# Rows of x and of the second norm turned by VectorE's block transpose and DRAM instead of TensorE

## The chip, the cores and the metric

The kernel runs on one core of a Trainium2 chip. The metric is the device time of one execution in microseconds, the median of several runs. The core's engines have a list of instructions each, worked off in order: TensorE (PE; PEld are its weight loads), VectorE (DVE), ScalarE (ACT), GpSimd (POOL) and SyncE (SP), which issues most DMAs. Lists wait for each other only by semaphores.

## The reference, cut to what matters

One layer of a hybrid decoder on 16 meta tokens and 1024 rows of x, width 1024, all in float32:

```python
u = rmsnorm(h, g_pre_mix)
z = u @ w_in                        # q, k, v, x_rec, y_rec
attn = sliding_window_attention_with_sinks(q, k, v, sinks)
hr = rg_lru(causal_depthwise_conv(xr), ...)
rec = gelu(yr) * hr
h = h + rmsnorm(concat(attn, rec) @ w_out, g_post_mix)
u = rmsnorm(h, g_pre_ffn)           # the second norm
f = square(relu(u @ w_ff1)) @ w_ff2
h = h + rmsnorm(f, g_post_ffn)      # returned without the meta tokens
```

`rmsnorm(x, g)` is x times the reciprocal root of its row's mean square, times g. Both products that begin with `u @` sum over the 1024 columns of u, so u is needed with its columns on the partitions: each tile of 128 rows has to be turned after its norm.

## The kernel before, in words

Each float32 operand of a matmul is split in a high and a low half (`split`, lines 96 and 99: ScalarE's copy to the matmul type, then VectorE's difference), and each product is three matmuls (`mm3`, lines 125, 130, 131): high by high, high by low, low by high.

**The first norm.** The 1040 rows go through in four pieces (`ALL`: 272, then three of 256). `normed` scales the rows of a piece: ScalarE's Square with a row sum (line 254), the reciprocal root as an addition and a power on GpSimd (`rstd_of`, lines 170 and 176), VectorE's multiplication (line 260). `transposed` then turns each of the 8 column blocks by TensorE against the identity into PSUM (line 357), and `split_scaled` multiplies by gamma out of PSUM into the two halves of u (lines 117 and 118). `project` multiplies a piece by a chunk of `w_in` for k, v, q and x_rec; the sinks take the sums from PSUM to SBUF.

**The second norm.** After the attention and the recurrence, `out_mm` forms the product with `w_out` for row tile t (0 to 7) in two PSUM banks. `out_norm` normalises it (Square on ScalarE, line 944; scaling on VectorE, line 950), adds x (line 953), writes the new residual to the output in DRAM (line 954), and scales it by its own norm (lines 956 and 958). `u2_tiles` turns that tile by 8 transposes (line 970) and multiplies by gamma out of PSUM, four blocks on ScalarE (line 981) and four on VectorE (line 975), into `u2f`: per half of four row tiles, four tiles of [128, 2, 512].

**The first feed-forward product** is one level of a fast matrix scheme on 2 by 2 blocks. `operand` splits tiles of `u2f`; `p1` and `p2` are its first products, on the first half of rows (tiles 0 to 3), and are spread between the last tiles' work; `t_sums` forms differences and sums of both halves (`t3`, `t2`), which need all eight tiles, and splits t2 (`ot2`). In the loop that follows, `product(ya[p], wa[p][1], ot2, ...)` is the first use of it. `early` and `prep_a` load and split the weights.

**Order.** The program is written in one order, and the scheduler of the tile framework places each engine's instructions from estimated times; `behind` and `chained` fix a few of them by hand. Buffers come from pools by tag with a fixed count (`raw` 2, `ws` 5, `d` 4, `c` 8 and so on), so a load waits for the last user of its buffer. SP's list holds the loads, the output's writes and, after the change, the trips through DRAM, in one order.

Of the kernel before, what the change touches and what calls it, by code (L numbers as in the profile page):

```python
# [9 lines left out]
F32 = mybir.dt.float32  # L10
# [27 lines left out]
def hybrid_layer(  # L38
# [311 lines left out]
    def transposed(b, xn, after=None):  # L350
        t0, n = ALL[b]
        for kc in range(KC):
            flip[0] += 1
            pt = bank(("pt", "o", "s")[flip[0] % 3])
            o = 0
            for s, m in xn:
                ins = nc.tensor.transpose(
                    pt[:, o : o + m], s[:m, kc * P : (kc + 1) * P], ident[:m, :m]
                )
# [12 lines left out]
            if b == 0:  # L372
                chained(0, high[0])
                chained(1, high[1])

    def fetch(cols, tag="raw", pieces=1):
# [540 lines left out]
    t4_dram = dpool.tile([P, 2, 4, 512], F32, name="t4_dram")  # L917

    u2f = [[None] * 4 for _ in range(2)]

    def out_mm(t, po, kcs):
        half, o = t // 4, (t % 4) * P
# [8 lines left out]
                )  # L931

    def out_banks(t):
        tag = ("pt", "o", "acc", "s", "pt", "acc", "s", "pt")[t]
        return [bank(tag), bank(tag)]

    def out_norm(t, po):
        xr = slot("d", [P, D])
        nc.sync.dma_start(xr, x[t * P : (t + 1) * P, :])
        h = slot("raw", [P, D])  # L940
        ssq = [small.tile([P, 1], F32, name=f"sq{n}", tag=f"sq{n}") for n in range(2)]
        for n in range(2):
            c = slice(512 * n, 512 * n + 512)
            nc.scalar.activation(
                h[:, c], po[n], AF.Square, scale=RMS_SC, accum_out=ssq[n]
            )
        rs = rstd_of(ssq)
        for n in range(2):
            c = slice(512 * n, 512 * n + 512)
            nc.vector.scalar_tensor_tensor(  # L950
                h[:, c], po[n], rs, gmix_b[:, c], op0=ALU.mult, op1=ALU.mult
            )
        nc.vector.tensor_tensor(h, h, xr, op=ALU.add)
# [4 lines left out]
        nc.vector.tensor_scalar(xr, h, rs2, None, op0=ALU.mult)  # L958
        return xr

    def u2_tiles(t, xn):
        half = t // 4
        if u2f[half][0] is None:
            u2f[half] = [slot("c", [P, 2, 512]) for _ in range(4)]
        o = (t % 4) * P
        for k4 in range(0, KC, 4):
            pt = bank("o", (P, 4, P))
            for i in range(4):
                kc = k4 + i
                nc.tensor.transpose(pt[:, i, :], xn[:, kc * P : (kc + 1) * P], ident)  # L970
            for i in range(0, 4, 2):
                kc = k4 + i
                dst = u2f[half][kc // 2]
                if k4:
                    nc.vector.tensor_tensor(
                        dst[:, :, o : o + P], pt[:, i : i + 2, :],
                        g_ffn_col[:, kc : kc + 2].to_broadcast([P, 2, P]), op=ALU.mult,
                    )
                    continue
                for n in range(2):  # L980
                    nc.scalar.activation(
                        dst[:, n, o : o + P], pt[:, i + n, :], AF.Copy,
                        scale=g_ffn_col[:, kc + n : kc + n + 1],
                    )

# [9 lines left out]
    def combine(dst, x0, x1, op):  # L995
        return nc.vector.tensor_tensor(dst, x0, x1, op=op).ins  # L996

    def operand(tiles):
        pairs = []
        for t_ in tiles:  # L1000
            hi, lo = pair("b", [P, 2, 512])
            split(hi, lo, t_)
            pairs.append((hi, lo))
        return pairs

# [106 lines left out]
    for t in range(8):  # L1112
        po = pos[t] if t < 4 else out_banks(t)
        out_mm(t, po, range(6 if t < 4 else 0, KC))
        for t_ in {4: (0,), 5: (2,), 6: (4,), 7: (5,)}.get(t, ()):
            u2_tiles(t_, xns[t_])
        xns[t] = out_norm(t, po)
        for t_ in {4: (1,), 5: (3,), 7: (6,)}.get(t, ()):
            u2_tiles(t_, xns[t_])
        if t == 4:  # L1120
            a11_early.update(early(0, 0, pair("a", ESH)))
        if t == 5:
            b11 = operand(u2f[0][0:2])
# [7 lines left out]
        p1(p, a11_early[p])  # L1131
    for p in range(2):
        p2(p, a12_early[p])
    t3 = [slot("a", [P, 2, 512]) for _ in range(2)]
    t2 = [slot("a", [P, 2, 512]) for _ in range(2)]
    ot2 = [pair("b", [P, 2, 512]) for _ in range(2)]

    def t_sums(c):
        for i in range(2):
            combine(t3[i][:, :, c], u2f[1][2 + i][:, :, c], u2f[1][i][:, :, c], ALU.subtract)  # L1140
            combine(t2[i][:, :, c], t3[i][:, :, c], u2f[0][i][:, :, c], ALU.add)
            hi, lo = ot2[i]
            split(hi[:, :, c], lo[:, :, c], t2[i][:, :, c])
# [9 lines left out]
    p2(2, a12_early[2])  # L1153
    ot3 = [pair("b", [P, 2, 512]) for _ in range(2)]
    for i in range(2):
        behind(urgent, split(*ot3[i], t3[i]))
    wa[1] = prep_a(1, urgent)


    def t_rest(k):  # L1160
        i = k % 2
        if k < 2:
            behind(mark[0], combine(u2f[1][i], u2f[1][i], u2f[0][i], ALU.subtract))
        elif k < 4:
            behind(mark[0], combine(t2[i], u2f[0][2 + i], t2[i], ALU.subtract))
        else:
            hl = pair("a", [P, 2, 512])
            late = mark[0]
            behind(late, split(*hl, t2[i]))
# [339 lines left out]
```

## Time and profile before

| what | us |
|---|---|
| median of 3 runs | 955.24 (955.24 to 955.97) |
| the profiled execution, its span | 955.3 |
| TensorE busy | 943.8 (99%) |
| VectorE busy | 655.7 (69%) |
| ScalarE busy | 505.9 (53%) |
| GpSimd busy | 129.1 (14%) |

The page lists the span as the profiled execution's time, and no other beside it. In rows of instructions the first number is the start in us from the span's start, the second the time to the end of the row's group; a group's row has a count, the busy us and mean ns of one, and the idle time in front with the engine that ended it. A row of a stretch lists busy time and instructions of PE, PEld, DVE, ACT and POOL, then TensorE's granted clock, the DMA engines' share and GB/s. A row of DMA issues gives the count, KB each and median us from issue to landing.

### The profile page before, as it was taken

Reading aid. Unit: us, or ns where it says so; the run is one execution under the profiler, and the core shown is the slowest. Engines: PE = TensorE matmul, PEld = TensorE weight load, DVE = VectorE, ACT = ScalarE, POOL = GpSimd, SP = SyncE. Lnnn points to the kernel's source line nnn. Section 1 sums busy time; section 2 is a strip of 40 time slices with the busy share of each in tenths; the row PEclk is TensorE's granted clock in tenths of the full one; section 3 lists DMA queues with packets and bytes.
Section 4 is the critical chain, followed back from the end, with each engine's and each line's share of the span. In section 5 each row is a group of like instructions: output and inputs, shape, how many; then the busy total and the mean of one; then the engine's idle time right before and its main releaser. Section 6 shows DMA issues by size and latency. Waiting matters only on the chain.

```text
span 955.3 us, 12432 instructions
## 1 busy us (share of the span) xinstructions
PE 943.8 (99%) x4728; PEld 789.7 (83%) x4728; DVE 655.7 (69%) x845; ACT 505.9 (53%) x854; POOL 129.1 (14%) x189
## 2 busy tenths in 40 slices
PE   9999999999999999999999999999999999999996
PEld 8999999877888878888888888888887788888885
DVE  6567987788856787665644465476667576779893
ACT  7537766568645554444655575654433343446441
POOL 4102563520021100010000000001121100001201
PEclk9999999999999999999999999999999999999999
DMA  8221010204226368674422364334777765647934
GB/s 271 56 67 23 24 45 24 67 23 131 83 109 185 133 220 264 198 253 144 155 89 88 111 203 127 104 113 114 175 180 186 185 199 177 192 139 196 246 65 89
DMA packets 88199, 130.21 MB, mean 136 GB/s; under 512 B 13702, under 2 KB 52630, under 8 KB 88140
## 3 DMA queue, kind: packets, MB, share of 16 engines
q1 hardware_dynamic: 78972, 104.44, 34.0%
q0 software_dynamic: 8880, 24.19, 12.2%
q8 instruction: 37, 0.61, 0.3%
q10 hardware_dynamic: 288, 0.79, 0.2%
q14 instruction: 22, 0.18, 0.1%
HBM read 109.93 MB, written 18.87 MB: 135 GB/s over the span
## 4 chain that ended last, share of the span: by engine, by line
PE 88%; DVE 5%; ACT 3%; DMA 2%; POOL 1%; issue 1%; SPq 0%; DVEq 0%; ACTq 0%; POOLq 0%
PE ps_acc L130 10%; PE ps_acc L131 10%; PE ps_acc L125 10%; PE ps_s L131 6%; PE ps_s L130 6%; PE ps_s L125 6%; PE ps_pt L130 6%; PE ps_pt L131 6%; PE ps_pt L125 6%; PE ps_o L130 5%; PE ps_o L131 5%; PE ps_o L125 5%; ACT c L82 1%; PE ps_o L691 1%; PE ps_acc L282 1%
## 5 line engine op out<-in xcount | busy, mean ns | idle before, releaser
L99 DVE TENSOR_TENSOR ws<-raw,ws 128x1024 fp32r<-128x1024 f32 (+1 forms) x69 | 82.6, 1197 | 76.1 <-ACT ws L96 24.3
L96 ACT CAST ws<-raw 128x1024 fp32r<-128x1024 f32 (+1 forms) x68 | 69.7, 1026 | 87.9 <-PE ps_o L130 23.9
L96 ACT CAST ws<-e 128x1024 fp32r<-128x1024 f32 x41 | 43.0, 1049 | 82.8 <-PE ps_o L130 35.3
L125 PE MATMUL ps_acc<-a,ws 128*128 128x256 f32 (+2 forms) x256 | 85.8, 335 | 0.0
L130 PE MATMUL ps_acc<-a,ws 128*128 128x256 f32 (+2 forms) x256 | 85.5, 334 | 0.0
L131 PE MATMUL ps_acc<-a,ws 128*128 128x256 f32 (+2 forms) x256 | 85.0, 333 | 0.0
L99 DVE TENSOR_TENSOR b<-b,b 128x1024 fp32r<-128x1024 f32 (+2 forms) x50 | 58.9, 1177 | 24.8 <-PE ps_o L130 19.1
L96 ACT CAST b<-b 128x1024 fp32r<-128x1024 f32 (+2 forms) x49 | 49.9, 1019 | 46.4 <-DVE b L996 41.0
L99 DVE TENSOR_TENSOR ws<-e,ws 128x1024 fp32r<-128x1024 f32 x41 | 50.1, 1223 | 32.4 <-ACT ws L96 18.9
L680 POOL TENSOR_SCALAR_AFFINE_SELECT c<-c 128x512 fp32r<-128x512 f32 x64 | 53.6, 858 | 67.6 <-ACT c L96 59.3
L125 PEld LDWEIGHTS ps_acc<-a,ws 128*128 128x128 f32 x256 | 48.3, 189 | 4.7 <-issue 0.2
L131 PEld LDWEIGHTS ps_acc<-a,ws 128*128 128x128 f32 x256 | 48.3, 189 | 4.5
L130 PEld LDWEIGHTS ps_acc<-a,ws 128*128 128x128 f32 x256 | 48.2, 188 | 4.4 <-issue 0.4
L125 PE MATMUL ps_acc<-ws,b 128*128 128x512 f32 (+1 forms) x120 | 46.3, 387 | 1.1 <-ACT ws L96 1.1
L130 PE MATMUL ps_acc<-ws,b 128*128 128x512 f32 (+1 forms) x120 | 46.3, 386 | 0.5 <-DVE ws L99 0.4
L131 PE MATMUL ps_acc<-ws,b 128*128 128x512 f32 (+1 forms) x120 | 46.1, 385 | 0.0
L125 PE MATMUL ps_pt<-ws,b 128*128 128x512 f32 x112 | 44.4, 396 | 0.0
L130 PE MATMUL ps_pt<-ws,b 128*128 128x512 f32 x112 | 44.1, 394 | 0.0
L131 PE MATMUL ps_pt<-ws,b 128*128 128x512 f32 x112 | 44.0, 393 | 0.0
L125 PE MATMUL ps_s<-ws,b 128*128 128x512 f32 x110 | 43.4, 395 | 0.0
L131 PE MATMUL ps_s<-ws,b 128*128 128x512 f32 x110 | 43.3, 394 | 0.0
L130 PE MATMUL ps_s<-ws,b 128*128 128x512 f32 x110 | 43.3, 393 | 0.0
(416 smaller groups left out, 2662.0 us busy)
## 6 DMA issues: line engine op xcount, KB each, us to landing
raw<-in_w_ff_dram SPq DMA_DIRECT2D x61, 512.0 KB, 4.1
e<-in_w_ff_dram SPq DMA_DIRECT2D x45, 512.0 KB, 4.0
a<-in_w_ff_dram SPq DMA_DIRECT2D x12, 512.0 KB, 6.6
s_dram<-a POOLq DMA_DIRECT2D x12, 512.0 KB, 3.7
c<-in_x_dram SPq DMA_DIRECT2D x8, 512.0 KB, 4.0
raw<-in_w_in_dram SPq DMA_DIRECT2D x8, 512.0 KB, 3.7
d<-in_x_dram SPq DMA_DIRECT2D x8, 512.0 KB, 3.3
out_dram<-raw SPq DMA_DIRECT2D x8, 512.0 KB
```

The lines of the kernel that those rows point to most:

```text
L82: ins = nc.scalar.activation(*args, **kwargs).ins
L96: nc.scalar.copy(hi, src)
L99: low = nc.vector.tensor_tensor(lo, src, f32(hi), op=ALU.subtract).ins
L125: ins = nc.tensor.matmul(dst, lh, rh, start=start, stop=False, skip_group_check=True).ins
L130: nc.tensor.matmul(dst, lh, rl, start=False, stop=False, skip_group_check=True)
L131: last_mm[0] = nc.tensor.matmul(dst, ll, rh, start=False, stop=stop, skip_group_check=True).ins.name
L282: last_mm[0] = nc.tensor.matmul(acc[:, :n], w[k // 2][:, kc, :], u[kc][k % 2][:, t0 : t0 + n], start=k == 0 and kc == 0, stop=k == last an ...
L680: nc.gpsimd.affine_select(out=p_[:, :, s], in_=f32(p_[:, :, 0]), pattern=[[0, 4], [g, P]], compare_op=op, fill=0.0, base=0, channel_multip ...
L691: nc.tensor.matmul(po[:, oc : oc + n], v, p_[:, pc : pc + n], start=first and k == 0, stop=last and k == 1, skip_group_check=True,)
```

## The change

Three helpers are new. `blocks` turns a scaled tile of 128 by 1024 on VectorE: the hardware turns blocks of 32 by 32, and the read takes every fourth column, so that what lands on one partition goes to DRAM in one run of 4 KB. `unblock` reads it back with the partition that the turned layout wants. `norm_blocks`, `read_blocks` and `split_blocks` use them for the third and fourth piece of x (row tiles 4 to 7), two reads per tile; the first two pieces stay on TensorE. In the second norm, tiles 0 to 6 are multiplied by gamma while they are scaled, against a copy of gamma on every partition (`gpre_b`, one of the five `ws` buffers), turned, written and read back by four reads straight into `u2f`; tile 7 stays on TensorE. `u2f`, t2 and t3 now have the shape [128, 16, 2, 32], and the splits reorder runs of 32 elements (`rows`). The last tile's product moves from the banks `pt` to `o`, which the transposes had used.

```diff
+    def blocks(y, src, dram):
+        nc.vector.transpose(
+            y.rearrange("p (b k t) -> p b k t", b=4, k=KC),
+            src.rearrange("p (k d b) -> p b k d", k=KC, b=4),
+        )
+        nc.sync.dma_start(dram.rearrange("a (d b) r -> (a d) (b r)", b=4), y)
+
+    def unblock(dst, dram, i, n):
+        w = 2 * P // n
+        nc.sync.dma_start(
+            dst.rearrange("p a k t -> p a (k t)"),
+            dram[:, :, w * i : w * i + w].rearrange("a p r -> p a r"),
+        )
+
+    def norm_blocks(b):
+        for i in (2 * b, 2 * b + 1):
+            src, y = xt[i], slot("d", [P, D])
+            ssq = small.tile([P, 1], F32, name="ssq", tag="ssq")
+            nc.scalar.activation(y, src, AF.Square, scale=RMS_SC, accum_out=ssq)
+            rs = rstd_of([ssq])
+            nc.vector.tensor_scalar(src, src, rs, None, op0=ALU.mult)
+            blocks(y, src, x_dram[i - 4])
+
+    def read_blocks(b):
+        for h in range(2):
+            for i in range(2):
+                unblock(turned(b, h)[:, 4 * i : 4 * i + 4], x_dram[2 * b + i - 4], h, 2)
+
+    def split_blocks(b):
+        t0, n = ALL[b]
+        for kc in range(KC):
...
+            split_scaled(
+                uh, ul, turned(b, kc // 4)[:, :, kc % 4], g_mix_col[:, kc : kc + 1]
+            )
...
-        if b:
-            transposed(b, xn if b == 1 else normed(b), done[b])
+        if b == 1:
+            transposed(b, xn, done[b])
+        elif b:
+            split_blocks(b)
+        if b in (1, 2):
+            norm_blocks(b + 1)
+            read_blocks(b + 1)
...
+    LAST_BY_DMA = 6
+    u2_dram = dpool.tile([LAST_BY_DMA + 1, 4, P, 2 * P], F32, name="u2_dram")
+    gpre_b = slot("ws", [P, D])
+    nc.scalar.dma_start(gpre_b, g_pre_ffn[0].partition_broadcast(P))
...
-        tag = ("pt", "o", "acc", "s", "pt", "acc", "s", "pt")[t]
+        tag = ("pt", "o", "acc", "s", "pt", "acc", "s", "o")[t]
...
-        nc.vector.tensor_scalar(xr, h, rs2, None, op0=ALU.mult)
-        return xr
+        if t > LAST_BY_DMA:
+            nc.vector.tensor_scalar(xr, h, rs2, None, op0=ALU.mult)
+            return xr
+        nc.vector.scalar_tensor_tensor(
+            xr, h, rs2, gpre_b, op0=ALU.mult, op1=ALU.mult
+        )
+        blocks(slot("d", [P, D]), xr, u2_dram[t])
...
+    def u2_read(t):
+        g = slice(4 * (t % 4), 4 * (t % 4) + 4)
+        for i, dst in enumerate(u2_half(t // 4)):
+            unblock(dst[:, g], u2_dram[t], i, 4)
...
-        for t_ in {4: (0,), 5: (2,), 6: (4,), 7: (5,)}.get(t, ()):
-            u2_tiles(t_, xns[t_])
         xns[t] = out_norm(t, po)
-        for t_ in {4: (1,), 5: (3,), 7: (6,)}.get(t, ()):
-            u2_tiles(t_, xns[t_])
+        if t:
+            u2_read(t - 1)
...
-    t_sums(slice(0, 3 * P))
+    t_sums(slice(0, 12))
     wa[0] = prep_a(0)
     u2_tiles(7, xns[7])
-    t_sums(slice(3 * P, 4 * P))
+    t_sums(slice(12, 16))
```

More of the change, by code (lines that the diff above doesn't have):

```diff
@@ L374, in transposed, with turned @@
                 chained(1, high[1])
+    def blocks(y, src, dram):
[10 more added lines that the diff above has]
+        )
+    x_dram = dpool.tile([4, 4, P, 2 * P], F32, name="x_dram")
+    def norm_blocks(b):
[6 more added lines that the diff above has]
+            blocks(y, src, x_dram[i - 4])
+    def turned(b, h):
+        return xt[2 * b + h].rearrange("p (g k t) -> p g k t", k=4, t=32)
+    def read_blocks(b):
[5 more added lines that the diff above has]
+        for kc in range(KC):
+            uh, ul = (
+                v[:, t0 : t0 + n].rearrange("p (g t) -> p g t", t=32) for v in u[kc]
+            )
+            split_scaled(
+                uh, ul, turned(b, kc // 4)[:, :, kc % 4], g_mix_col[:, kc : kc + 1]
+            )
     def fetch(cols, tag="raw", pieces=1):
@@ L957, in out_norm, with u2_half @@
         rs2 = rstd_of([ssq2])
-        nc.vector.tensor_scalar(xr, h, rs2, None, op0=ALU.mult)
-        return xr
+        if t > LAST_BY_DMA:
[3 more added lines that the diff above has]
+            xr, h, rs2, gpre_b, op0=ALU.mult, op1=ALU.mult
+        )
+        blocks(slot("d", [P, D]), xr, u2_dram[t])
+    def u2_half(half):
+        if u2f[half][0] is None:
+            u2f[half] = [slot("c", [P, 16, 2, 32]) for _ in range(4)]
+        return u2f[half]
+    def u2_read(t):
+        g = slice(4 * (t % 4), 4 * (t % 4) + 4)
+        for i, dst in enumerate(u2_half(t // 4)):
+            unblock(dst[:, g], u2_dram[t], i, 4)
     def u2_tiles(t, xn):
[L962 to L965, printed above, removed]
+        g = slice(4 * (t % 4), 4 * (t % 4) + 4)
         for k4 in range(0, KC, 4):
@@ L972, in u2_tiles @@
                 kc = k4 + i
[L973 to L979, printed above, removed]
-                for n in range(2):
[L981 to L984, printed above, removed]
+                dst = u2_half(t // 4)[kc // 2]
+                for n in range(2):
+                    d_ = dst[:, g, n]
+                    s_ = pt[:, i + n, :].rearrange("p (a t) -> p a t", a=4)
+                    col = g_ffn_col[:, kc + n : kc + n + 1]
+                    if k4:
+                        nc.vector.tensor_scalar(d_, s_, col, None, op0=ALU.mult)
+                    else:
+                        nc.scalar.activation(d_, s_, AF.Copy, scale=col)
     w1v = w_ff1.rearrange("(b k p) c -> b p k c", b=2, p=P)
@@ L996, in combine, with rows @@
         return nc.vector.tensor_tensor(dst, x0, x1, op=op).ins
+    def rows(tile_, c=slice(0, 16)):
+        return tile_.rearrange("p k (g t) -> p g k t", t=32)[:, c]
     def operand(tiles):
@@ L1001, in operand @@
             hi, lo = pair("b", [P, 2, 512])
-            split(hi, lo, t_)
+            split(rows(hi), rows(lo), t_)
             pairs.append((hi, lo))
@@ L1133, in hybrid_layer @@
         p2(p, a12_early[p])
-    t3 = [slot("a", [P, 2, 512]) for _ in range(2)]
-    t2 = [slot("a", [P, 2, 512]) for _ in range(2)]
+    t3 = [slot("a", [P, 16, 2, 32]) for _ in range(2)]
+    t2 = [slot("a", [P, 16, 2, 32]) for _ in range(2)]
     ot2 = [pair("b", [P, 2, 512]) for _ in range(2)]
@@ L1139, in t_sums @@
         for i in range(2):
-            combine(t3[i][:, :, c], u2f[1][2 + i][:, :, c], u2f[1][i][:, :, c], ALU.subtract)
-            combine(t2[i][:, :, c], t3[i][:, :, c], u2f[0][i][:, :, c], ALU.add)
+            combine(t3[i][:, c], u2f[1][2 + i][:, c], u2f[1][i][:, c], ALU.subtract)
+            combine(t2[i][:, c], t3[i][:, c], u2f[0][i][:, c], ALU.add)
             hi, lo = ot2[i]
-            split(hi[:, :, c], lo[:, :, c], t2[i][:, :, c])
-    t_sums(slice(0, 3 * P))
+            split(rows(hi, c), rows(lo, c), t2[i][:, c])
+    t_sums(slice(0, 12))
     wa[0] = prep_a(0)
     u2_tiles(7, xns[7])
-    t_sums(slice(3 * P, 4 * P))
+    t_sums(slice(12, 16))
     urgent = mark[0]
@@ L1155, in hybrid_layer @@
     for i in range(2):
-        behind(urgent, split(*ot3[i], t3[i]))
+        behind(urgent, split(*map(rows, ot3[i]), t3[i]))
     wa[1] = prep_a(1, urgent)
@@ L1168, in t_rest @@
             late = mark[0]
-            behind(late, split(*hl, t2[i]))
+            behind(late, split(*map(rows, hl), t2[i]))
             for n in range(2):
```

## The prediction

> **What bounds the kernel now.** I read the busy times and the chain that ended last, then busy time by stretch, then the instructions in order of time around the two stages that the change touches, then single groups and DMA times.
>
> ```profile
> PE 943.8 (99%) x4728; PEld 789.7 (83%) x4728; DVE 655.7 (69%) x845; ACT 505.9 (53%) x854; POOL 129.1 (14%) x189
> PE 88%; DVE 5%; ACT 3%; DMA 2%; POOL 1%; issue 1%; SPq 0%; DVEq 0%; ACTq 0%; POOLq 0%
> 20.00:40.00 20.00, 20.00 (x170) 19.64 (x169) 13.77 (x30) 12.06 (x30) 5.11 (x13) 1.00 0.31 81
> 320.00:340.00 20.00, 20.00 (x100) 16.56 (x99) 17.56 (x29) 13.16 (x28) 2.40 (x4) 1.00 0.66 211
> 340.00:360.00 20.00, 19.94 (x86) 15.79 (x85) 15.97 (x26) 10.52 (x17) 1.61 (x3) 1.00 0.56 184
> ```
>
> TensorE is busy 99% at full clock (1.00). A matmul removed is worth its issue slot if nothing else was awaited there, and a wait put in front of TensorE is lost for good, because it has no idle time later to catch up. VectorE is the near second: 17.56 of 20 us in the stretch where the second norm's last tiles become operands.
>
> **The transposes removed.** Per tile of 128 rows TensorE issues 8. Tiles 4 to 7 of x lose 32, tiles 0 to 6 of the second norm 56, in all 88.
>
> ```profile
> 319.31 0.39 PE L131 MATMUL ps_pt<-a,b 128*128 128x512 f32 x1
> 319.54 1.03 PE L970 MATMUL ps_o<-ident,d 128*128 128x128 f32 x8
> 320.33 0.48 PE L125 MATMUL ps_acc<-b,a 128*128 128x512 f32 x1
> 320.64 0.39 PE L130 MATMUL ps_acc<-b,a 128*128 128x512 f32 x1
> ```
>
> Products of 512 columns start 0.23 us apart (319.31, 319.54). Without the transposes the product of 320.64 would have started at 319.77, so 8 transposes cost 0.87 us, 0.109 each, and 88 cost 9.6 us: the largest possible gain, 945.7 us. The Trainium skill ("TensorE: Matmul & The Clock Gate", Part 4) gives some 275 ns for a transpose in a kernel; by that the 88 would be worth 24 us, as an estimate. The trace has that duration (1.03 us ends 0.27 after the last start) but overlaps them, so the step of 0.109 is what counts.
>
> **The x pieces.** Some transposes were free already.
>
> ```profile
> 32.67 0.27 PE L357 MATMUL ps_s<-ident,d 128*128 128x128 f32 x1
> ...
> 33.43 0.38 PE L357 MATMUL ps_o<-ident,d 128*128 128x128 f32 x2
> 33.56 0.36 PE L125 MATMUL ps_acc<-a,ws 128*128 128x256 f32 x1
> 33.05 0.37 ACT L464 COPY c<-ps_acc 128x256 f32<-128x256 f32 x1
> ```
>
> The q product at 33.56 needs the bank that ScalarE's copy of v leaves at 33.42. The 9 transposes in front of it run inside that wait, and the next piece has 8 at the same place. So 17 of 32 are worth nothing; 15 x 0.109 = 1.6 us is gained.
>
> Against it stands VectorE's order. In the changed program its list has the first block transpose right behind the sinks of k of the first piece, ahead of these:
>
> ```profile
> 22.84 0.62 DVE L437 TENSOR_TENSOR ws<-ps_acc,ws 64x144 fp32r<-64x144 f32 x2
> 23.50 1.23 DVE L348 TENSOR_TENSOR ws<-e,ws 128x1024 fp32r<-128x1024 f32 x1
> 25.73 0.48 DVE L118 SCALAR_TENSOR_TENSOR a<-ps_pt,gcol,a 128x256 fp32r<-128x256 f32 x1
> 24.78 1.27 PE L282 MATMUL ps_acc<-a,ws 128*128 128x272 f32 x8
> 26.47 0.36 PE L130 MATMUL ps_acc<-a,b 128*128 128x256 f32 x1
> ```
>
> TensorE's work at 24.78 waits for the low weights that end at 24.73, and that of 26.47 for the first low half of u (26.21). Both move by one block transpose, T.
>
> No row shows T. Bounds from rows of as many columns:
>
> ```profile
> L958 DVE TENSOR_SCALAR d<-raw,rs 128x1024 f32<-128x1024 f32 x8 | 6.0, 754 | 12.8 <-POOL rs L176 12.8
> L953 DVE TENSOR_TENSOR raw<-raw,d 128x1024 f32<-128x1024 f32 x8 | 9.8, 1224 | 0.2
> L851 DVE TENSOR_TENSOR_SCAN c<-b,c 128x1040 f32<-128x1040 f32 x2 | 4.6, 2314 | 0.0
> L1343 DVE SCALAR_TENSOR_TENSOR a<-b,rs,ws 128x1024 f32<-128x1024 f32 x4 | 5.1, 1279 | 0.0
> L975 DVE TENSOR_TENSOR c<-ps_o,gcol 128x256 f32<-128x256 f32 x16 | 6.0, 415 | 0.0
> ```
>
> Fastest 0.75, slowest 2.31; I take 1.22, what most f32 operations of this size take here. So the second piece starts 1.2 us later.
>
> Its u must also be back from DRAM. VectorE turns tile 5 by 31.6 at T = 1.22 (the first low halves end 1.2 later, then a scaling of 0.75 and T); then DMAs:
>
> ```profile
> s_dram<-a POOLq DMA_DIRECT2D x12, 512.0 KB, 3.7
> d<-in_x_dram SPq DMA_DIRECT2D x8, 512.0 KB, 3.3
> raw<-in_w_in_dram SPq DMA_DIRECT2D x8, 256.0 KB, 3.3
> ```
>
> Write 3.7, two reads of 256 KB 3.3 and an issue of 0.4: 39.0 or somewhat later, while TensorE comes to the piece near 40. VectorE reaches its first low half about 0.3 us late. Tiles 6 and 7 have 10 us more. Sum of the x pieces at T = 1.22: -1.6 + 1.2 + 0.3 = -0.1 us. At 0.75: -0.6. At 2.31: VectorE, with four turns and q's sink ahead of those halves, comes 2.0 late: +2.7. The ScalarE and VectorE halves of u keep their count. SP's gate loads queue behind the new DMAs, but are needed only after the attention.
>
> **The second norm.** Each of seven tiles adds on VectorE T and a scaling with gamma of 1.28 for 0.75, and drops two evictions of 0.415: at T = 1.22 a net 0.9 us per tile. ScalarE loses four copies per tile. Four reads of 128 KB in 256-byte runs per tile are added on SP; I take 4.5 us for them, 3.3 and three issues of 0.4. One broadcast of gamma on ScalarE's queue lands long before it is used. The chain of the first tiles:
>
> ```profile
> 269.25 0.76 DVE L958 TENSOR_SCALAR d<-raw,rs 128x1024 f32<-128x1024 f32 x1 [2.12 <-POOL rs L176]
> 270.07 1.41 DVE L950 SCALAR_TENSOR_TENSOR raw<-ps_o,rs,e 128x512 f32<-128x512 f32 x2
> 271.52 1.23 DVE L953 TENSOR_TENSOR raw<-raw,d 128x1024 f32<-128x1024 f32 x1
> 274.92 0.75 DVE L958 TENSOR_SCALAR d<-raw,rs 128x1024 f32<-128x1024 f32 x1 [2.10 <-POOL rs L176]
> ```
>
> The period is 5.67 us with 2.1 idle, waiting for Square and power. The new turn stands ahead of the residual add (L953), not in the idle time, so the period becomes 1.28 + 1.41 + T + 1.23 + 2.1 = 7.2. On SP, tiles 2 to 7's loads of x now stand behind reads that wait for a write (3.7): T turns late, 1 to 2 us more at one or two tiles. Tile 3 is scaled at 292 instead of 286.24, its reads land near 304, and the eight operand splits of tiles 0 to 3 end near 312. None of this stops TensorE: it has the out products of tiles 4 to 7, which end at 315.1 (40 transposes' 4.4 us before 319.54).
>
> Then cover runs out. In the changed order TensorE has 72 products (p1(0), p1(1), p2(0), p2(1), p1(2), p1(3)), tile 7's 8 transposes, two products of p2(2), the first with t2, then ten of p2(2). From 315 that is 16.6 us to the transposes (331.5) and 0.9 + 0.5 to t2 at 332.9. What t2 and p2(2) need, before:
>
> ```profile
> 326.59 0.75 DVE L958 TENSOR_SCALAR d<-raw,rs 128x1024 f32<-128x1024 f32 x1 [0.46 <-POOL rs L176]
> 341.35 0.39 PE L131 MATMUL ps_pt<-b,a 128*128 128x512 f32 x1
> 341.58 0.40 PE L125 MATMUL ps_acc<-b,e 128*128 128x512 f32 x1
> L996 DVE TENSOR_TENSOR a<-c,c 128x768 f32<-128x768 f32 x2 | 1.9, 950 | 0.0
> L996 DVE TENSOR_TENSOR raw<-raw 128x512 f32<-128x512 f32 x16 | 10.9, 688 | 0.3
> L99 DVE TENSOR_TENSOR a<-raw,a 128x1024 fp32r<-128x1024 f32 x6 | 7.3, 1212 | 2.7 <-ACT a L96 2.7
> ```
>
> Tile 7 is scaled near 332 (VectorE's list from tile 4 on takes that long; ScalarE's Square of tile 7 also stands behind the activation of p2(1)'s block, which TensorE finishes at 326). Behind that scaling VectorE has, up to the low half of p2(2)'s weights: five operations of 512 columns (0.69), four new evictions of 128 (0.3, under the 0.415 of 256), five of 768 (0.95), four of 256 (0.42) and one of 1024 (1.21): 12.3 us, 11 with the 0.08 by which neighbours overlap, and 0.6 for a cast: done at 343.6. TensorE waits from 332.9, some 10.7 us. (Those weights cannot come before about 338 in any case: their load waits for tile 7's row to be written out.) It then owes ten products of p2(2), 2.3 us, and is at 345.9 where before it was at 341.8 (p2(2) complete, first t2 product out). So the stage loses 4.1 us, the 6.1 of its 56 transposes being in it already. At T = 0.75 tile 7 comes no earlier than 331.6: +3.7. At T = 2.31 four or five turns are uncovered, tile 7 comes near 337: +9.
>
> **Sum**, against the execution's span of 955.3, equal to the median of 955.24 within 0.1: -0.1 + 4.1 = +4.0, that is 959.3 us. Bounds: 955.3 - 0.6 + 3.7 = 958.4 and 955.3 + 2.7 + 9 = 967.
>
> **Rivals.**
> A slow block transpose. Each read steps over 16 bytes, and if that costs two cycles an element, the price is the scan's 2.31: 967 us. No row of this case reads with such a step, so nothing speaks against it. The Trainium skill ("SBUF — State Buffer", Door 1: The DMA port swizzle) says that SBUF has lines of 16 bytes and that each access to a new line pays a penalty. A step of four f32 is just such an access; no run here shows it yet.
>
> Faster: the cover holds. If VectorE's list behind tile 7 and the load of p2(2)'s weights end by 333 rather than 343.6, the 6.1 us stay, with 1.6 less at most 1.2 in x: 955.3 - 6.1 - 0.4 = 948.8, at best 945.7. It decides at 339.5, where wait and transposes balance. For it: VectorE still has 2.4 us idle in 320 to 340 and loses evictions. Against it: one list in order, where even 1 us of T does not remove the five sums of 768.
>
> Even: only half of that wait comes, 955 to 957.
>
> **Chances.** Forecast 0.46 (own range 957 to 963), slow turn 0.27, cover holds 0.19, even 0.08. A change of 0.2% is about what a measurement tells here: 953.3 to 957.2 is no change. Faster 0.19, same 0.05, slower 0.76. The range 952.5 to 967.5 leaves out most of the cover's case and a tail of the slow one.
>
> **What would show it.** T from its own group. TensorE without L357 after the second piece but with a wait before it near 26; the period of the second norm's first tiles at 7.2 us; a TensorE wait near 332 of about 10 us, released by VectorE's split or ScalarE's cast for p2(2) and t2. The forecast is wrong if TensorE stays at 20.00 in the stretch 320 to 340, or if VectorE's operations on 32-element runs cost more than the 1.21 of contiguous ones.

## The result, and the profile after

The changed kernel takes 977.25 us (median of 4 runs, 974.10 to 982.00) against 955.24 us (955.02 to 955.97): ratio 1.023, with a 95% interval of 1.020 to 1.026. It is 22 us slower, where 4 us had been forecast and no case went beyond 967. The profiled execution of it took 974.1 us, with a span of 972.4 us, 17.1 more than before. It was the fastest of the four, so the sums of waits below account for 17 of the 22 us.

From the page of the changed kernel, busy times and the chain that ended last:

```profile
PE 940.6 (97%) x4640; PEld 784.3 (81%) x4640; DVE 674.1 (69%) x844; ACT 498.9 (51%) x826; POOL 128.7 (13%) x189
PE 81%; DVE 6%; DMA 5%; ACT 3%; issue 2%; POOL 1%; SPq 1%; DVEq 0%; ACTq 0%; POOLq 0%
```

The three stretches of the changed kernel that the prediction showed of the one before:

```profile
20.00:40.00 20.00, 17.86 (x145) 16.83 (x144) 17.90 (x28) 10.99 (x27) 5.55 (x15) 1.00 0.60 175
320.00:340.00 20.00, 18.40 (x77) 13.94 (x76) 16.34 (x17) 7.80 (x16) 3.47 (x6) 1.00 0.71 220
340.00:360.00 20.00, 6.23 (x17) 4.55 (x18) 17.31 (x29) 11.53 (x19) 1.74 (x3) 0.58 0.88 275
```

TensorE's share of the chain fell from 88% to 81%, and DMA has 5% of it. In 340 to 360 us TensorE works 6.23 of 20 us, and for what it does there it was granted 0.58 of its clock. Before, it was 1.00 in all three stretches.

TensorE's waits in the changed kernel, longest first (what waited, for whom, us in all, times, longest):

```profile
PE ps_o L1035 <- DVE d L1012: 7.0, 1, 7.0
PE ps_pt L125 <- ACT a L96: 6.1, 1, 6.1
PE ps_acc L125 <- ACT c L508: 3.6, 1, 3.6
PE ps_acc L282 <- DVE ws L348: 1.8, 1, 1.8
...
PE ps_pt L131 <- DVE a L99: 1.3, 1, 1.3
```

Three of them are in the second norm (7.0 before tile 7's transposes, 6.1 and 1.3 at the first weights behind them), two in the x pieces (3.6 and 1.8). With the small ones they are 24.4 us. The same view of the kernel before begins with this one:

```profile
PE ps_acc L308 <- DVE base_e L562: 1.5, 1, 1.5
```

All its waits together are 4.1 us. To the 20.3 us of difference comes the low clock, 4.3 us (busy time times what is missing to 1.00: 1.3 in 50 to 60 us, 3.0 in 340 to 370 us). Against them stand 71 to 88 removed transposes of 0.109 us, 7.7 to 9.6 (by the prediction 17 of the 88 had stood inside a wait). The sum, 15.0 to 16.9, comes near the 17.1 of the span.

The block transposes and the residual add of the changed kernel, by group:

```profile
L378 DVE STREAM_TRANSPOSE d<-d 128x1024 f32<-128x1024 f32 x7 | 14.0, 2003 | 0.0
L378 DVE STREAM_TRANSPOSE d<-c 128x1024 f32<-128x1024 f32 x4 | 8.1, 2019 | 0.1
L1006 DVE TENSOR_TENSOR raw<-raw,d 128x1024 f32<-128x1024 f32 x8 | 9.8, 1224 | 6.8 <-DMA d<-in_x_dram 6.7
```

VectorE in the changed kernel, in order of time: the scalings of tiles 0 and 1, the add and the scaling of tile 2, and the scaling of tile 7:

```profile
275.01 1.29 DVE L1014 SCALAR_TENSOR_TENSOR d<-raw,rs,ws 128x1024 f32<-128x1024 f32 x1 [2.12 <-POOL rs L176]
282.79 1.29 DVE L1014 SCALAR_TENSOR_TENSOR d<-raw,rs,ws 128x1024 f32<-128x1024 f32 x1 [2.10 <-POOL rs L176]
289.74 1.23 DVE L1006 TENSOR_TENSOR raw<-raw,d 128x1024 f32<-128x1024 f32 x1 [2.44 <-DMA d<-in_x_dram]
293.14 1.29 DVE L1014 SCALAR_TENSOR_TENSOR d<-raw,rs,ws 128x1024 f32<-128x1024 f32 x1 [2.10 <-POOL rs L176]
345.54 0.75 DVE L1012 TENSOR_SCALAR d<-raw,rs 128x1024 f32<-128x1024 f32 x1 [0.46 <-POOL rs L176]
```

A turn takes 2.00 us, not 1.22. The first period of the second norm is 7.78 us (275.01 to 282.79), the next 10.35 (to 293.14), because tile 2's add waits 2.44 us for its load of x. Over the eight tiles the periods are between 7.8 and 12.3 us, and tile 7 is scaled at 345.54 instead of 326.59. Of these 19.0 us, 5.8 are there from the first tile on, which is scaled at 275.01 instead of 269.25: that is the lateness of the x pieces. The longest period, 12.3 us, has no wait for a load of x in it, and the kernel before has one of 12.9 us one tile later (305.49 to 318.37).

### The profile page after: what moved, and what is told of

Its sections match the earlier page's. It is cut to its first block, busy times and chain, and to the rows that moved or that the text cites. A ratio compares the mean times of both kernels' runs of the same rounds, so it can differ in the third digit from the quotient of the medians.

```text
span 972.4 us, 12310 instructions
## 1 busy us (share of the span) xinstructions
PE 940.6 (97%) x4640; PEld 784.3 (81%) x4640; DVE 674.1 (69%) x844; ACT 498.9 (51%) x826; POOL 128.7 (13%) x189
## 4 chain that ended last, share of the span: by engine, by line
PE 81%; DVE 6%; DMA 5%; ACT 3%; issue 2%; POOL 1%; SPq 1%; DVEq 0%; ACTq 0%; POOLq 0%
PE ps_acc L130 10%; PE ps_acc L125 9%; PE ps_acc L131 9%; PE ps_s L131 6%; PE ps_s L130 6%; PE ps_s L125 5%; PE ps_pt L131 5%; PE ps_pt L130 5%; PE ps_pt L125 5%; PE ps_o L130 5%; PE ps_o L131 5%; PE ps_o L125 5%; PE ps_o L740 1%; DMA x_dram<-d 1%; DMA d<-in_x_dram 1%
## 5 line engine op out<-in xcount | busy, mean ns | idle before, releaser
L125 PEld LDWEIGHTS ps_acc<-a,ws 128*128 128x128 f32 x256 | 49.0, 191 | 9.3 <-ACT c L508 4.0
L131 PEld LDWEIGHTS ps_acc<-a,ws 128*128 128x128 f32 x256 | 49.0, 191 | 4.5
L130 PEld LDWEIGHTS ps_acc<-a,ws 128*128 128x128 f32 x256 | 49.0, 191 | 4.4 <-issue 0.4
L130 PE MATMUL ps_pt<-ws,b 128*128 128x512 f32 x110 | 43.4, 395 | 0.0
L131 PE MATMUL ps_pt<-ws,b 128*128 128x512 f32 x110 | 43.3, 394 | 0.0
L125 PE MATMUL ps_pt<-ws,b 128*128 128x512 f32 x110 | 43.2, 393 | 0.0
```

The source lines that it names most:

```text
L125: ins = nc.tensor.matmul(dst, lh, rh, start=start, stop=False, skip_group_check=True).ins
L130: nc.tensor.matmul(dst, lh, rl, start=False, stop=False, skip_group_check=True)
L131: last_mm[0] = nc.tensor.matmul(dst, ll, rh, start=False, stop=stop, skip_group_check=True).ins.name
```

## The experiments

All ratios are to the kernel before, run on the same chip, with 95% intervals. Where several changes are in a run, its diff shows only what is new against the run named.

### Each part alone

The change was cut in two at the second norm: the one run has the new functions and the loop over the pieces of x, and all from `u2f` on as before; the other has x as before and the new second norm.

> Only the pieces 2 and 3 of x go by VectorE's block transposes and DRAM; the second norm is that of the kernel before. In the profile of the changed kernel the first scale of the out norm's chain (the ms of tile 0) stands 5.8 us later than before. Theory A (the two parts' losses add up, since TensorE has no idle time later that could take up the first): 955.2 + 5.8 = 961.0 us, 959.5 to 962.5. Rival B (the lateness is taken up before the second norm, or the x stage disturbs only through the second norm): 954.5 to 957 us.

> Only tiles 0 to 6 of the second norm go by block transposes and DRAM; x is turned by TensorE as before. Theory A (the parts add up): 977.3 - 5.8 = 971.5 us, 969 to 973. Rival B (the second norm's chain is late mainly because the x stage delivers late): under 966 us.

x alone: 963.89 us (961.30 to 968.23), ratio 1.009 (1.006 to 1.012). The second norm alone: 970.57 us (967.82 to 972.75), ratio 1.015 (1.013 to 1.018). The losses are 8.4 and 15.0 us, together 23.4, against 22.0 of both: within the intervals they add up, as theory A had it. But x alone is 1.4 us above theory A's range: it costs 8.4 and not the 5.8 that the profiled execution of the changed kernel showed. A stretch of the run with x alone:

```profile
50.00:60.00 10.00, 6.91 (x38) 6.91 (x39) 4.54 (x19) 3.73 (x10) 0.00 (x0) 0.66 0.01 2
```

ScalarE and TensorE of that run in order of time, in front of that stretch and at its begin:

```profile
48.58 2.50 ACT L117 ACTIVATE a<-c,gcol 128x256 fp32r<-128x256 f32 x6 [3.53 <-DMA c<-x_dram]
50.98 0.73 ACT L477 CAST b<-ps_acc 64x256 fp32r<-64x256 f32 x2
51.73 0.91 ACT L117 ACTIVATE a<-c,gcol 128x256 fp32r<-128x256 f32 x2
52.67 0.37 ACT L508 COPY c<-ps_acc 128x256 f32<-128x256 f32 x1
53.09 0.58 PE L125 MATMUL ps_acc<-a,ws 128*128 128x256 f32 x1 [4.32 <-ACT c L508]
```

ScalarE's list has six of the eight splits of piece 3 (L117), which wait for the reads from DRAM, ahead of the sinks that empty piece 2's banks (L477, the copy of k; L508, that of v). The data come at 48.58, the bank of v is free at 53.04, and TensorE stands 4.3 us. Its granted clock over the stretch of 50 to 60 us is 0.66.

### The turn, read contiguously

```diff
-            src.rearrange("p (k d b) -> p b k d", k=KC, b=4),
+            src.rearrange("p (b k d) -> p b k d", k=KC, b=4),
```

> The same instructions and DMAs as the changed kernel, but each block transpose reads its 32-element runs contiguously instead of with a step of four; the columns then arrive in another order, so the result is that of a permuted operand and only the time is read. Theory S (the step of four makes the block transpose slow): its mean falls from 2.00 us to about 1.2 us, and with 7 turns in the second norm's chain at 0.8 us each and 1.5 us in the x stage the time falls to 968 to 972 us. Rival C (an fp32 block transpose costs 2.0 us however it reads): mean 1.95 to 2.05 us, and the time stays at 975 to 979 us.

978.14 us (975.28 to 978.56), ratio 1.023 (1.021 to 1.025). The group of the second norm's turns in this run, and tile 2's add:

```profile
L378 DVE STREAM_TRANSPOSE d<-d 128x1024 f32<-128x1024 f32 x7 | 8.7, 1239 | 0.0
290.57 1.23 DVE L1006 TENSOR_TENSOR raw<-raw,d 128x1024 f32<-128x1024 f32 x1 [3.45 <-DMA d<-in_x_dram]
```

Theory S is right about the turn and wrong about the time: the step of four costs 0.76 of the 2.00 us, and without it the kernel is not measurably faster. So the turn's price is not what the 22 us are made of. It must stand in front of something that is late anyway, and the second line shows what: tile 2's add now waits 3.45 us for its load of x, where it waited 2.44 behind the slow turns.

### The loads of x ahead of the reads

SP's list in the changed kernel, in order of time:

```profile
287.33 0.33 SPq L382 DMA_DIRECT2D u_dram<-d  x1
290.99 0.34 SPq L1007 DMA_DIRECT2D out_dram<-raw  x1
291.42 2.57 SPq L386 DMA_DIRECT2D c<-u_dram  x4
294.04 0.50 SPq L992 DMA_DIRECT2D d<-in_x_dram  x1
```

The load of x (L992) for the tile after next stands behind the four reads (L386) of a turned tile, and these wait for its write (L382) to land and take 2.6 us to issue. Hence a loop: turn, write, reads, load of x, add, Square, scaling, turn. This run puts the reads of a tile behind the load of x for the tile two further on:

```diff
+        if n == 4:                # in unblock
+            behind(x_load[0], ins)
...
-        nc.sync.dma_start(xr, x[t * P : (t + 1) * P, :])
+        x_load[0] = nc.sync.dma_start(xr, x[t * P : (t + 1) * P, :]).ins.name
...
         xns[t] = out_norm(t, po)
-        if t:
-            u2_read(t - 1)
+        if t > 1:
+            u2_read(t - 2)
...
+    u2_read(6)
```

> The changed kernel, with one change of order on SP's queue: in the second norm the four reads of a turned tile are put behind the load of x for the tile two further on, so that no load of x waits for a write to DRAM to land. Theory Q (the period of 8 to 12 us is the loop turn, write, wait for the landing, reads, load of x, add): the waits of VectorE's adds for x go (2.4, 1.0, 2.5 and 0.8 us in the profile of the changed kernel), tile 7 is scaled 6 to 10 us sooner, TensorE's wait of 7.0 us before tile 7's transposes falls under 2 us, and the time falls to 966 to 971 us. Rival V (VectorE's and ScalarE's own list with turns of 2.0 us sets the period): 975 to 979 us, and the wait stays.

972.46 us (968.92 to 973.34), ratio 1.016 (1.014 to 1.019): 4.8 us less than the changed kernel. VectorE's scalings of tiles 0 to 2 in this run:

```profile
277.44 1.28 DVE L1018 SCALAR_TENSOR_TENSOR d<-raw,rs,ws 128x1024 f32<-128x1024 f32 x1 [2.12 <-POOL rs L176]
285.22 1.28 DVE L1018 SCALAR_TENSOR_TENSOR d<-raw,rs,ws 128x1024 f32<-128x1024 f32 x1 [2.10 <-POOL rs L176]
293.01 1.29 DVE L1018 SCALAR_TENSOR_TENSOR d<-raw,rs,ws 128x1024 f32<-128x1024 f32 x1 [2.10 <-POOL rs L176]
```

The adds wait for no load any more and the first four periods are 7.78 to 7.84 us, so the loop was there. The three behind them stay at 10.4 to 11.9 us, so the loop did not make those. The time is 1.5 us above theory Q's range. Tile 7 is scaled at 342.02, 3.5 us sooner and not 6 to 10 (tile 0 was 2.4 us later than in the changed kernel's profile). TensorE's wait before tile 7's transposes fell only to 2.6 us, and behind them one of 7.5 us for the cast of the first sums stands in place of the 6.1 and 1.3.

### The turn again, with the loop out

The same contiguous read, in the run with the loads ahead.

> The run with x's loads ahead of the reads, with the block transposes reading contiguously (1.24 us instead of 2.00; the columns arrive in another order, only the time is read). In the run with x's loads ahead the period of the first tiles is 7.78 us, and it is VectorE's list: 1.28 + 1.40 + 2.00 (turn) + 1.18 + 0.1 and 2.1 of wait for rs. Theory T (once the loop through SP is out, the turn's length counts in full): a period of 7.0 us for tiles 1 to 4, and the time falls by 3 to 5 us, to 967 to 970 us. Rival Z (the turn's length does not count here either, as it did not in the changed kernel): 971 to 974 us.

968.73 us (966.90 to 972.91), ratio 1.014 (1.011 to 1.017), 3.7 us less than with the loads ahead alone by the medians, though the two intervals overlap. The scalings come at 274.68, 281.71, 289.07 and 296.12, periods of 7.0 to 7.4 us. The periods bear theory T out: the turn's length sets them as soon as VectorE's list, and not SP's, does. What it is worth in the kernel's time these two runs leave open.

### The turn behind the next tile's add

```diff
-        blocks(slot("d", [P, D]), xr, u2_dram[t])
+        turn.append((xr, u2_dram[t]))
...
         add = nc.vector.tensor_tensor(h, h, xr, op=ALU.add).ins.name
+        if turn:
+            behind(add, blocks(slot("e" if t < 7 else "d", [P, D]), *turn.pop()))
```

> The run with x's loads ahead of the reads, with each turn also put behind the add of the next tile on VectorE, so that it lies in the 2.1 us in which VectorE waited for rs; to have the buffers for it, the turned tile goes to another slot. Theory T (period = 1.28 + 1.40 + 1.18 + 0.1 + a wait of at least 2.1 that now holds the turn, near 5.9 us): tile 4's scale comes 7 to 8 us sooner than in the run with the loads ahead, the long waits of TensorE at 340 to 355 us shrink by some 6 us, and the time falls to 962 to 967 us. Rival V (from tile 5 on the splits of W1 and of the operands, 4 by 1.22 us and more, set the pace, and the head start is lost there): 970 to 973 us.

970.39 us (968.27 to 971.06), ratio 1.015 (1.012 to 1.017): by the medians 2.1 us less than with the loads ahead alone, with intervals that overlap. That is in rival V's range and above theory T's. VectorE in this run:

```profile
280.45 2.04 DVE L378 STREAM_TRANSPOSE e<-d 128x1024 f32<-128x1024 f32 x1
282.70 1.28 DVE L1021 SCALAR_TENSOR_TENSOR d<-raw,rs,ws 128x1024 f32<-128x1024 f32 x1 [0.17 <-POOL rs L176]
294.29 2.00 DVE L378 STREAM_TRANSPOSE e<-d 128x1024 f32<-128x1024 f32 x1 [1.55 <-DMA u_dram<-e]
```

The turn now fills the wait for rs (0.17 is left of 2.1), and the first periods are 6.0 and 6.2 us. But one buffer of `e` serves all turned tiles, so a turn waits for the write of the one before (1.55), and tile 7 is scaled at 336.97, 5 us sooner than with the loads ahead alone. TensorE then waits 8.8 us for the cast of the first sums, so the head start is lost there.

### Piece 2's sinks ahead of piece 3's splits

In the run with x alone:

```diff
+            pair_ = split_scaled(uh, ul, turned(b, kc // 4)[:, :, kc % 4], ...)
+            if b == 3:
+                for name, ins in zip(freed, pair_):   # copy of v, low half of k
+                    behind(name, ins)
```

> The run with x alone by DRAM, with one change of order: ScalarE's copy of piece 2's v out of PSUM, and VectorE's low half of piece 2's k, are put ahead of the splits of piece 3, which wait for the reads from DRAM. Theory L (TensorE stood still for 4.3 us at 48.8 because that copy was queued behind splits that waited for a transfer, and then ran 10 us at a granted clock of 0.66): the wait falls under 1.5 us, the clock in 50 to 60 us is above 0.9, and the time falls from 963.9 us to 956 to 959 us. Rival D (the data of piece 3 are late, whatever the order): a wait for the splits takes the place of the wait for the copy, and the time stays at 962 to 965 us.

957.90 us (956.90 to 961.57), ratio 1.0015 (0.9996 to 1.0034): 6.0 us less than x alone by this order alone, as theory L had it. What is left, 1.6 us against the kernel before on this chip, cannot be told from zero. ScalarE and TensorE in this run:

```profile
48.72 0.37 ACT L514 COPY c<-ps_acc 128x256 f32<-128x256 f32 x1
48.99 3.31 ACT L117 ACTIVATE a<-c,gcol 128x256 fp32r<-128x256 f32 x8
49.15 0.38 PE L125 MATMUL ps_acc<-a,ws 128*128 128x256 f32 x1 [0.65 <-ACT c L514]
```

The copy of v ends before the splits begin, TensorE waits 0.65 instead of 4.3 us, and the clock in 50 to 60 us is 1.00.

### All three orders

The second norm with its two changes of order and x with its one.

> The three changes of order together: x's loads ahead of the reads, each turn behind the next tile's add, and piece 2's copies out of PSUM ahead of piece 3's splits. The x part's order was worth 6.0 us by itself. Theory A (the parts add up): 6 us under the run with the turn behind the add, 956 to 961 us, and the changed kernel's loss is then gone but for 1 to 5 us. Rival B (they overlap, since tile 7 is set by its own list): no more than 3 us under that run.

965.01 us (963.11 to 968.81), ratio 1.008 (1.006 to 1.010): 5.4 us under the run with the turn behind the add. The parts add up, but the sum ends 4 us above theory A's range, since that run itself had missed. TensorE still waits 9.3 us for the cast of the first sums.

### Idle products in the waits

The products 2 and 3 of the first W1 rows are issued ahead of tile 7's transposes, and TensorE multiplies into a bank that nobody reads, 26 times before the transposes and 22 times behind them; the control does so once at each place.

```diff
+    first = filler(26, "o", last_mm[0])
+    u2_tiles(7, xns[7], first)
+    second = filler(22, "pt", last_mm[0])
```

> The changed kernel, in which TensorE runs 26 idle products (128x512, into a bank nobody reads) between the last product with tiles 0 to 3 and tile 7's transposes, and 22 more between those and the first product of the third W1 pair: 48 by 0.23 us is 11 us of the 13 us that it stood idle there. The products 2 and 3 of W1's first rows are put ahead of the transposes in the program, where TensorE ran them anyhow. Theory K (after an idle stretch TensorE's granted clock is low for some us: 0.58 in 340 to 360 us): with the idle stretches filled the clock there is above 0.9, the products behind them start 0.23 us apart instead of 0.43 us, and the time falls by 2 to 4 us against the run with one idle product in each place. Rival N (the low clock is only what a half idle stretch shows, or the idle products delay real ones): within 1 us of that run, or slower.

> The control of the run before: the same program with one idle product in each of the two places instead of 26 and 22. Both theories: that of the changed kernel, 974 to 979 us, with a granted clock near 0.6 in 340 to 360 us.

978.76 us (975.92 to 980.90) with them and 977.31 us (974.61 to 981.71) in the control; ratios 1.024 (1.021 to 1.026) and 1.023 (1.020 to 1.026). No gain: the 1.4 us between them are within the intervals, as rival N had it, and theory K's 2 to 4 us did not come. Three stretches of the run with idle products:

```profile
340.00:350.00 10.00, 10.00 (x42) 8.05 (x41) 7.29 (x9) 3.24 (x4) 1.56 (x3) 0.91 0.88 295
350.00:360.00 10.00, 6.77 (x33) 5.09 (x31) 9.97 (x19) 6.02 (x12) 0.65 (x1) 0.94 0.92 291
360.00:370.00 10.00, 9.20 (x30) 7.36 (x31) 9.97 (x15) 4.64 (x9) 0.00 (x0) 0.72 0.18 53
```

While TensorE is kept busy its clock is 0.91 and 0.94 there, against 0.78 and 0.50 in the same two stretches of the control. But tile 7's transposes went out no sooner (349.97 against 347.95 in the control), for they wait for VectorE, and the waits of 1.5 and 2.5 us that remained behind the idle products were again followed by a low clock (0.72). The run shows that the low clock follows waits; what filling them rightly would be worth stays open.

### Which tiles go through DRAM

First, x as before and tiles 0 to 3 alone by DRAM, with the changed kernel's order.

```diff
-    LAST_BY_DMA = 6
+    LAST_BY_DMA = 3
+        for t_ in {6: (4,), 7: (5,)}.get(t, ()):
+            u2_tiles(t_, xns[t_])
         xns[t] = out_norm(t, po)
```

> x is turned by TensorE as before; of the second norm only tiles 0 to 3 go by block transposes and DRAM, and tiles 4 to 6 are turned by TensorE at the places of the kernel before: 32 transposes go, 3.5 us at 0.109 us each. Theory Q (the loss of the second norm is the loop through SP's queue, which here ends with tile 3, while tiles 4 to 7 have slack): 951 to 956 us. Rival E (the lateness of tiles 0 to 3, some 3 to 4 us each, is carried on to tile 7): 960 to 968 us.

963.56 us (962.00 to 965.06), ratio 1.008 (1.006 to 1.009), as rival E had it. The lateness of four tiles is carried on: tile 7 is scaled at 335.42, and the add of tile 4 still waits 2.73 us for its load behind reads.

Then x as before and both orders of the second norm mended, with tiles 0 to 6, 0 to 5 and 0 to 3 through DRAM (`LAST_BY_DMA` 6, 5 and 3). In the last two, and in the run above, TensorE turns the other tiles at their old places, and tile 7's product goes to the banks `pt` again.

> x by TensorE as before; tiles 0 to 6 of the second norm by block transposes and DRAM with both changes of order (x's loads ahead of the reads, each turn behind the next tile's add). All theories: the run with all three changes of order less the 1.5 us that x then still cost, 961 to 966 us. It is the control for the two runs beside it.

> The run beside it with tile 6 turned by TensorE at the place that the kernel before has, so that only tiles 0 to 5 go through DRAM. Theory W (what is left of the loss is the trip of the last tile by DRAM: turn, write, wait for the landing, four reads and their landing, some 10 to 12 us before the sums of tiles 4 to 6 can begin, with W1's loads behind those reads on SP): the 8 to 9 us for which TensorE waits for the operand's cast shrink to under 5 us, and the time falls by 3 to 6 us against the run beside it. Rival V (VectorE's list from tile 5 on, with splits of 1.22 us each, is late whatever tile 6 does): within 1.5 us of it.

> The same with tiles 4 to 6 turned by TensorE at the places that the kernel before has; only tiles 0 to 3, needed 17 us and more later, go through DRAM, with both changes of order. 32 transposes at 0.109 us are gone, 3.5 us. Theory W (only the trips of the late tiles and the two orders cost): tile 7 is scaled within 2 us of the kernel before, TensorE has no wait over 2 us in 300 to 360 us, and the time is 952 to 956 us. Rival E (the lateness of tiles 0 to 3 is still carried on to tile 7, as in the run with tiles 0 to 3 and the old order, 963.6 us): 958 to 964 us.

| through DRAM | us | ratio | TensorE's longest wait in the stage |
|---|---|---|---|
| tiles 0 to 6 | 960.60 (959.37 to 964.05) | 1.005 (1.003 to 1.006) | 7.4 |
| tiles 0 to 5 | 956.52 (955.78 to 960.02) | 1.001 (0.999 to 1.002) | 2.4 |
| tiles 0 to 3 | 956.87 (955.12 to 959.54) | 1.0005 (0.9993 to 1.0016) | 1.8 |

SP, VectorE and TensorE of the run with tiles 0 to 6 through DRAM, in order of time:

```profile
326.21 0.33 SPq L382 DMA_DIRECT2D u_dram<-d  x1
326.60 0.43 SPq L1028 DMA_DIRECT2D d<-in_w_ff_dram  x1
...
330.13 2.53 SPq L387 DMA_DIRECT2D c<-u_dram  x4
331.55 0.69 DVE L1031 TENSOR_TENSOR d<-raw,d 128x512 f32<-128x512 f32 x1 [3.54 <-DMA d<-in_w_ff_dram]
...
336.06 0.95 DVE L1031 TENSOR_TENSOR a<-c,c 128x768 f32<-128x768 f32 x1
339.74 0.80 PE L125 MATMUL ps_acc<-b,e 128*128 128x512 f32 x1 [7.35 <-ACT b L96]
```

VectorE and TensorE of the run with tiles 0 to 5:

```profile
325.15 0.95 DVE L1031 TENSOR_TENSOR a<-c,c 128x768 f32<-128x768 f32 x1
336.06 0.50 PE L125 MATMUL ps_pt<-b,a 128*128 128x512 f32 x1 [2.40 <-ACT a L96]
```

TensorE of the run with tiles 0 to 3:

```profile
338.24 0.50 PE L131 MATMUL ps_pt<-b,a 128*128 128x512 f32 x1 [1.81 <-DVE a L99]
```

Tile 6 is turned by 326.2 and its reads are issued by 332.7, and the sums over tiles 4 to 6 (768 columns) begin at 336.06; with tile 6 on TensorE they begin at 325.15. A load of W1 also goes out right behind tile 6's write, at 326.60, and VectorE stands 3.54 us for it. Both are what theory W names, and tile 6 alone is worth 4.1 us. The run with tiles 0 to 6, 960.60 us, ended 0.4 us under the range expected of it.

Tiles 0 to 3 cost nothing that can be told from zero any more, but the 3.5 us of their 32 transposes are not gained either: the time is 0.9 us above theory W's range, although tile 7 is scaled at 326.89 and no wait is over 2 us. TensorE comes to the weights of p2(2) sooner and waits for VectorE's split of them, 1.81 us.

### The transposes issued twice

The kernel before, with each of the 88 transposes issued twice.

> The kernel before, in which each of the 88 transposes that the change removes is issued twice on TensorE, into the same place. It prices what the change could gain. Theory G (a transpose costs its step of 0.109 us, and those of the x pieces that stand in a wait cost nothing): 71 to 88 by 0.109 us, 7.7 to 9.6 us more, 963 to 966 us. Rival H (a transpose costs its whole duration of 0.27 us, as it would if they did not overlap): 88 by 0.27 us, 24 us more, near 979 us. Rival N (they are mostly hidden, by which the change never had much to gain): under 960 us.

967.10 us (966.40 to 969.29), ratio 1.012 (1.010 to 1.014): 11.0 us more, 9.8 to 13.1 by the interval, or 0.125 us each over 88. That is 1.4 us more than theory G's most and far from H. So a transpose added to the kernel before costs about what the prediction took for one removed. That one removed gives as much back is not shown: no run that removed transposes was faster than the kernel before.

## Why the prediction was wrong, point by point

Both terms of its sum were too small: x was taken at -0.1 us and measured 8.4 by itself, the second norm at 4.1 and measured 15.0. Each failed in what is queued behind a transfer, more than in the price of an instruction.

**The price of the transposes.** The step of 0.109 us held within 15% (0.125 measured when they are doubled, in the kernel before), and was not the error. The 24 us that the Trainium skill's figure gave ("TensorE: Matmul & The Clock Gate", Part 4: some 275 ns each) are refuted by that run; in the row of eight the transposes start 0.109 us apart, though each lasts 0.27.

**T, the length of a turn.** It was taken at 1.22 and measured 2.00, inside the bounds of 0.75 and 2.31. The prediction's own steps at 2.00, read between its two ends, would have given +1.9 for x and +7.6 for the norm, 965 us. But T is not the step that failed. With T at 1.24 the changed kernel takes as long as with 2.00. The rival of the slow turn was right that the step of four costs and wrong that this sets the time.

**The x pieces.** The first turn in front of the weights' low half was right: TensorE waits 1.8 us there. "Tiles 6 and 7 have 10 us more" is the step that failed. Piece 3's data came at 48.58 and TensorE to its piece near 48.8, so nothing was left of the 10 us. Its splits stood in ScalarE's list ahead of the sinks that free TensorE's banks; the prediction looked only at when the data are needed, not at what is queued behind the instruction that waits for them. Measured 8.4 us instead of -0.1, of which 6.0 are this order.

**The loads of x behind the reads.** The prediction saw the queue and sized it at "1 to 2 us more at one or two tiles". It is a loop through SP: the adds of tiles 2, 3, 4 and 7 wait 2.44, 0.96, 2.51 and 0.82 us, 6.7 in all, and the periods up to tile 4 grow to 10.8 us. Taking it out was worth 4.8 us. The period of 7.2 us from VectorE's list was the right formula: with T at 2.00 it gives 8.0, with the loop out 7.78 was measured, and at 1.24 it was 7.0 to 7.4.

**Tile 7.** "Tile 7 is scaled near 332" failed too: it was 345.54. The lateness of x is one part of it (5.8 us at tile 0; with x as before tile 7 came at 337.95), the loop another (342.02 with it out). That nothing stops TensorE before tile 7 held: the out products end near 321, which is the forecast 315.1 and the 5.8 of x. But TensorE then stood 7.0 us before tile 7's transposes, where the prediction had no wait. The list behind the scaling was right, 11.8 us measured from its scaling to the low half of p2(2)'s weights, 11.6 forecast. The waits came to 14.4 us (7.0, 6.1 and 1.3) instead of 10.7.

**The DRAM trip of the last tile** was not a term of the sum for the second norm. With both orders mended the sums with turned tile 6 begin 10 us after its turn, and W1's loads stand in the same queue. That was worth 4.1 us between the runs with and without tile 6.

**The clock.** The sum took every wait at its length, and so put the low clock behind it at nothing. In the changed kernel that adds 4.3 us.

The 32-element runs cost nothing, as forecast: the operand's splits took 1225 ns each against 1220 in the same group before. And the case that the cover holds was nearer than the changed kernel let one think: with two orders mended and tile 6 on TensorE the second norm costs 0.06% (-0.07 to 0.19), the same as before. No run was faster than the kernel before.

## What to carry to other kernels

Before a transfer is put into a list that is worked off in order, ask of every engine what stands behind the first instruction that waits for it: the sinks that free PSUM, the loads of the next tile, the weights. A trip through DRAM of some 10 us suits data that are needed much later (tiles 0 to 3 here) and not the last tile that everything waits for. And a wait of 2.2 us and more in front of TensorE cost more than its length here, so that a removed instruction of 0.1 us must not buy one.

## What the runs showed of the hardware

A block transpose of 128 by 1024 float32 took 1.24 us when it read contiguously and 2.00 us with a step of four. The Trainium skill ("SBUF — State Buffer", Door 1: The DMA port swizzle) says that an access that crosses to a new line of 16 bytes pays a penalty; a step of four float32 crosses at every element, and these two rows agree.

Behind the waits of 4.3 and 6.1 us TensorE issued at about half rate for 5 to 6 us. TensorE of the changed kernel in order of time, 4 to 7 us behind the wait of 6.1 us that ended at 354.45:

```profile
358.40 0.63 PE L130 MATMUL ps_pt<-b,a 128*128 128x512 f32 x1
358.83 0.63 PE L131 MATMUL ps_pt<-b,a 128*128 128x512 f32 x1
...
361.13 0.39 PE L130 MATMUL ps_acc<-b,e 128*128 128x512 f32 x1
361.36 0.39 PE L131 MATMUL ps_acc<-b,e 128*128 128x512 f32 x1
```

The products start 0.43 us apart and, from 360.45 on, 0.23. In the run with x alone the 24 products of 256 columns behind the wait of 4.3 us (53.09 to 58.38) took 0.21 us each instead of 0.12, some 2.3 us lost beside the wait. A wait of 1.8 us was followed by a full clock (tiles 0 to 3 through DRAM), one of 2.2 us by 0.83 in the next 10 us (in the run with piece 2's sinks ahead, near 759 us), where the half rate lasted some 3 us. The Trainium skill ("TensorE: Matmul & The Clock Gate", HAM oscillation — how this bites in real kernels) gives some 3.4 us of idle time as the border; here 2.2 us were enough.
